# Operands of TensorE moved to multiples of 128 bytes, a few products left out, and a square root by ScalarE, in a one-core decoder layer

## The chip, the core and the metric

The kernel runs on one core of a Trainium2 chip. Its engines work side by side, each on its own list of instructions, and wait for one another by semaphores: TensorE (PE in the profile) multiplies matrices, with PEld for its weight loads; VectorE (DVE) and ScalarE (ACT) do elementwise work; GpSimd (POOL) does very little here; SyncE (SP) issues nearly all DMAs. Operands of TensorE lie in SBUF, a memory of 128 partitions, and its results go to PSUM. The metric is the time of one execution in microseconds (us) on the device.

## What is computed

One layer of a hybrid decoder, for one sequence of 2,048 tokens of width 1,024 in float32. The core of the reference:

```python
u = rmsnorm(h, norm_mix_w)
proj = u @ w_in                                  # hq, hf, hi, hg, attention's q, k, v
f = lb + (1 - lb) * sigmoid(hf);  k = 1 - f      # 4 heads, 128 x 128 state
# S_t = diag(f_t) S_{t-1} + k_t v_t^T,  o_t = S_t^T q_t, the state starts as zeros
o_hg = rmsnorm(o_hg, hg_norm_w) * silu(hg)
o_att = sliding_window_attention_with_sinks(...) # 8 query heads, 2 key heads, window 128
h = h + concat(o_hg, o_att) @ w_out
v = rmsnorm(h, norm_ffn_w)
gate = causal_depthwise_conv(v @ w_gate) ;  h = h + (silu(gate) * (v @ w_up)) @ w_down
return rmsnorm(h, final_norm_w)
```

## The kernel before

**Stages.** The sequence is worked in two halves of 1,024 tokens (`hf` 0 and 1). Each half passes through four stages: mix (projections, recurrent heads, attention), the output projection, gate and up, and down. In time, by the profile: mix of half 0 to about 339 us, the output projection to 452, gate and up to 877, down to 1,086; in half 1 the output projection begins at 1,421, gate and up run from 1,534 to 1,959, down to 2,137, and the row blocks of the end to 2,172.

**Large products.** Every large product is made of three products of the type float32r: both factors are split into a high part (a rounded copy by ScalarE) and a low part (what is left, by VectorE), and hi·hi, hi·lo and lo·hi are added up in PSUM. Nearly all have 128 x 128 weights (the stationary operand, loaded by an LDWEIGHTS of its own for each matmul) and a moving operand of 128 x 512. `unit` (line 202) makes the projections, 48 matmuls in each of 52 units. `project_v` (lines 601 to 603) uses x as weights and moves 256 columns. Gate and up go two tiles at a time through `pair_unit` (lines 734 to 736), where seven products of quarters stand for eight (Strassen's scheme; 84 matmuls, 44 times); down does the same over 2,816 channels (lines 921 to 923), piece by piece (`prep_piece`).

**Small products.** The recurrent heads (`hgrn`) cut a half into eight chunks of 128 tokens. For each head they transpose K (`pkn`, line 541), make each chunk's update of the state from it (`pu`, line 548), run the state through the chunks on VectorE (`SS`, line 552; `state` holds what the half before left, line 587), and add for each chunk the product of ST with v (line 563) to that of Q with the state before the chunk (line 564). Attention makes its scores (`psc`, line 387, float32r, 256 columns) from query parts `qh`, `ql` and the keys `KS`. The other small products are plain float32; the trace shows each of those as two matmul records, and transposes as one.

**The end.** In half 1 the last product of down is made with rows of tokens as its output, so that the last RMSNorm can be done row block by row block (`last_rows`, four blocks `tb` of 128 tokens). Per block: ScalarE squares and sums (line 1034), VectorE forms the mean (`msr`), takes 1/sqrt from an integer first guess (lines 1038, 1039) and three Newton steps of two instructions (lines 1042, 1043), and scales the rows (line 1046), which a DMA writes out. For the last block ScalarE also scales `y1` (line 1050) by the same factor.

**Memory plan.** Pools are laid one behind another in SBUF, and each tile is rounded up to 32 bytes per partition. The constants begin at byte 2,176 with `nmw` (32 bytes), `ones` (512), `warm` (4, rounded to 32), `ident` (512), `state` (2,048), and end at 11,840; then come the pools x, w and h with tiles of 4,096 bytes, a pool of small tiles, and the pool of the stage. What follows from that, modulo 128 bytes:

| tiles | offset modulo 128 |
|---|---|
| XH, XL, xhd, xld, whi, wlo, hid, lod, the tiles of h; K, Q, ST, Kn, G, KS, V; nearly all of gate, up and down | 64 |
| `ga`: two slots of 2 + 1,024 float32 (4,104 bytes, rounded to 4,128) | 64 and 96 |
| `dd` of each half's first pair, behind the two slots of `ga` | 0 |
| v, SS, sc, qh, ql, po, pp: behind `F64`, a tile of 32 bytes | 32 |
| ones | 32 |

The tag `ga` holds the gate tiles, and it is borrowed twice: by the first pair of each half for Sh and Sl (their low part in the second slot), and by down for the weights of every third piece, `k % 3 == 1` (hi in the first slot, lo in the second; the profile calls them gad). In the same way `dd` holds the first pair's factor S4. Slices that a matmul takes from a tile start at multiples of 512 bytes, except in the levels of `hgrn`.

**Order.** Within each engine instructions run in the order in which they were issued. `ORDER` interleaves the steps of heads and attention by hand, `tc.issue_after` delays two places, and a planner (a scheduler that works with estimated costs) decides in the end which engine's instruction of which strand comes when.

Of the kernel before, what the change touches and what calls it, by code (L numbers as in the profile page):

```python
# [8 lines left out]
F32 = mybir.dt.float32  # L9
F32R = mybir.dt.float32r  # L10
U32 = mybir.dt.uint32
I32 = mybir.dt.int32
AF = mybir.ActivationFunctionType
ALU = mybir.AluOpType
# [3 lines left out]
P = 128  # L18
D = 1024
KT = D // P  # L20
S = 2048
HALF = 1024
NH = S // HALF
TT = HALF // P
# [6 lines left out]
EPS = 1e-6  # L31
PIECES = [2, 2, 2, 2, 2, 1]
OPS = ["B11", "T1", "B21", "T2", "T3", "B22", "T4"]
QUADS = ["A11", "A12", "A21", "A22"]
PRODUCTS = [("P1", "A11", "B11"), ("P5", "S1", "T1"), ("P6", "S2", "T2"), ("P3", "S4", "B22"),
            ("P7", "S3", "T3"), ("P2", "A12", "B21"), ("P4", "A22", "T4")]
AFTER = {2: 'po'}
ORDER = ("f0 q0 l0 qa0 v0 s0 sc0 w0 pv0 p0 f1 q1 l1 g0 pw0 w1 qa1 g1 sc1 f2 s1 q2 p1 qa2 m0 pv1 pw1 l2 v1 "
         "s2 sc2 f3 m5 q3 g2 p2 pv2 pw2 qa3 m6 m1 sc3 l3 m4 m2 s3 g3 pv3 p3 pw3").split()
UP_AFTER = 'T2'  # L40
LEVELS = [1, 2, 4, 8, 16, 32, 64]
# [7 lines left out]
def hymba_layer(ctx: ExitStack, tc: tile.TileContext, a: dict, out: bass.AP, rows_out: bass.AP):  # L49
    nc = tc.nc  # L50
# [6 lines left out]
    cp = pool("const")  # L57
# [18 lines left out]

    nmw = cp.tile([P, KT], F32, name="nmw")
    nc.scalar.dma_start(nmw, a["norm_mix_w"])
    ones = cp.tile([P, P], F32, name="ones")
    nc.vector.memset(ones, 1.0)  # L80
    warm = cp.tile([P, 1], F32, name="warm")
    nc.scalar.activation(warm, ones[:, 0:1], AF.Sigmoid)
# [4 lines left out]
    state = cp.tile([P, HG, P], F32, name="state")  # L87
    nc.vector.memset(state, 0.0)
    halo = cp.tile([P, FT, 2], F32, name="halo")
# [7 lines left out]
    marks = {}  # L97
# [350 lines left out]
    def hgrn(hf, h, X, invb, vs, WG, gates, mix, p, fu=None):  # L448

        fu = fu or unit(a["w_f"][h], X, "f")  # L450
        f = p.tile([P, HALF], F32, tag="f", name="f", bufs=2)
# [12 lines left out]
        Q = p.tile([P, HALF], F32, tag="Q", name="Q", bufs=2)  # L464
# [3 lines left out]
        ST = p.tile([P, TT, P], F32, tag="t4", name="ST", bufs=2)  # L468
# [23 lines left out]
        F = f  # L492
        for m in LEVELS:
# [26 lines left out]
            Fv = F.rearrange("p (b w) -> p b w", w=2)  # L520
            Fn = p.tile([P, nb], F32, tag=f"F{m}", name=f"F{m}", bufs=1)
            nc.vector.tensor_tensor(Fn, Fv[:, :, 0], Fv[:, :, 1], op=ALU.mult)
# [11 lines left out]
        v = vs[h]  # L534

        Kn = p.tile([P, TT, P], F32, tag="t4", name="Kn", bufs=2)
        for b in range(NB):
            pk = ps("hg", "pkn")
            for i in range(4):
                c = slice((b * 4 + i) * P, (b * 4 + i + 1) * P)  # L540
                nc.tensor.transpose(pk[:, i * P:(i + 1) * P], K[:, c], ident)
            nc.scalar.copy(Kn[:, 4 * b:4 * b + 4].rearrange("p a b -> p (a b)"), pk)
        SS = p.tile([P, TT, P], F32, tag="SS", name="SS", bufs=1)
        for b in range(NB):
            pu = ps("hg", "pu")
            for i in range(4):
                c = 4 * b + i
                marks["pu"] = nc.tensor.matmul(pu[:, i * P:(i + 1) * P], Kn[:, c], v[:, c], start=True, stop=True)
            for i in range(4):
                c = 4 * b + i  # L550
                prev = state[:, h] if c == 0 else SS[:, c - 1]
                nc.vector.scalar_tensor_tensor(SS[:, c], prev, F[:, c:c + 1], pu[:, i * P:(i + 1) * P],
                                               op0=ALU.mult, op1=ALU.add)
# [5 lines left out]
        for c in range(TT):  # L559
            cs = slice(c * P, (c + 1) * P)  # L560
            prev = state[:, h] if c == 0 else SS[:, c - 1]
            o = po[c // 4][:, c % 4 * P:(c % 4 + 1) * P]
            nc.tensor.matmul(o, ST[:, c], v[:, c], start=True, stop=False)
            marks["po"] = nc.tensor.matmul(o, Q[:, cs], prev, start=False, stop=True)
            nc.scalar.activation(on[:, c], o, AF.Square, accum_out=ss[:, c:c + 1])
# [8 lines left out]
        for b, bs in halves():  # L574
# [8 lines left out]
            if h == HG - 1:  # L583
                hi, lo = mix[h]
                nc.scalar.copy(hi[:, bs], g[:, bs])
                nc.vector.tensor_tensor(lo[:, bs], g[:, bs], hi[:, bs].bitcast(F32), op=ALU.subtract)
        nc.vector.tensor_copy(state[:, h], SS[:, TT - 1])
        yield
# [176 lines left out]
    def gate_up(hf, ops, hs, nxt, p):  # L765
# [5 lines left out]
        for pr in range(FT // 2):  # L771
            f0 = 2 * pr
            W, nxt = nxt, None
            ga = [p.tile([P, 2 + HALF], F32, tag="ga", name="ga", bufs=2) for _ in range(2)]

# [218 lines left out]
    def last_rows(hf, hh, st, fw, ready, pieces, p, then):  # L994
# [6 lines left out]
        def small(name):  # L1001
            return sp.tile([P, 1], F32, tag=name, name=name)

        for tb in range(4):
            ts = slice(tb * P, (tb + 1) * P)
# [30 lines left out]
            nc.vector.tensor_scalar(ms, ss, 1.0 / D, base[:, tb:tb + 1], op0=ALU.mult, op1=ALU.add)  # L1036
            yi = y.bitcast(I32)
            nc.vector.tensor_scalar(yi, ms.bitcast(I32), 1, None, op0=ALU.logical_shift_right)
            nc.vector.tensor_scalar(yi, yi, -1.0, float(0x5F3759DF), op0=ALU.mult, op1=ALU.add)
            nc.vector.tensor_scalar(mh, ss, -0.5 / D, half[:, tb:tb + 1], op0=ALU.mult, op1=ALU.add)  # L1040
            for _ in range(3):
                nc.vector.tensor_scalar(t, y, y, mh, op0=ALU.mult, op1=ALU.mult)
                nc.vector.tensor_scalar(y, t, 1.5, y, op0=ALU.add, op1=ALU.mult)
# [131 lines left out]
```

## Time and profile before

| | us |
|---|---|
| time, median of 3 runs (2181.68 to 2183.84) | 2183.36 |
| the profiled execution | 2181.92 |
| its span, first to last instruction | 2179.9 |
| mean granted TensorE clock in it | 0.999 |

The page gives, for each engine, the busy time, its share of the span and the number of instructions; then the chain of work that ended last; then groups of instructions with their count, total and mean duration. Matmuls overlap each other: the duration of one (0.39 us for 512 columns) is longer than the distance from its start to the start of the next. How fast TensorE works is therefore read in the timeline, from start to start. For VectorE and ScalarE a duration is what an instruction costs, nearly.

### The profile page before, as it was taken

The page shows a single profiled execution, that of the slowest core. Times are in us where ns is not written, and L with a number is a line of the kernel's source. Part 1 is how long each engine was busy: PE and PEld are TensorE (multiplying, and loading weights), DVE is VectorE, ACT ScalarE, POOL GpSimd, SP SyncE. Part 2 cuts the span into 40 slices and gives each one's busy share as a digit, 9 for nine tenths or more (in the row PEclk, how much of TensorE's full clock was granted, in tenths as well). Part 3 has the DMA queues.
Part 4 walks back from the last instruction along what each step waited for, and adds up shares of the span by engine and source line. Part 5 has one row for each costly group of instructions (what it writes and reads, how often), then busy time and mean ns, then how long its engine had stood idle before and what let it go on. Part 6 is the DMA issues. An engine that isn't in the chain of part 4 may idle for free.

```text
span 2179.9 us, 29020 instructions
## 1 busy us (share of the span) xinstructions
PE 2162.5 (99%) x11211; PEld 1813.3 (83%) x11211; DVE 1630.9 (75%) x2458; ACT 1049.7 (48%) x1825; POOL 15.8 (1%) x37
## 2 busy tenths in 40 slices
PE   8999999999999999999999999999999999999998
PEld 7988988888888888888889889888888888888887
DVE  6566668689787878785865666677888888787865
ACT  6445456554444445335635365445644444443452
POOL 2000000000000000000000000000000000000000
PEclk9999999999999999999999999999999999999999
DMA  4111112413232334964641010114232323259743
GB/s 156 40 30 39 30 39 69 135 59 126 92 115 93 99 118 152 384 227 152 205 135 30 30 49 22 50 61 143 70 116 87 129 84 124 86 190 393 232 145 131
DMA packets 91146, 254.41 MB, mean 117 GB/s; under 512 B 11136, under 2 KB 13952, under 8 KB 91008
## 3 DMA queue, kind: packets, MB, share of 16 engines
q1 hardware_dynamic: 90576, 252.29, 34.6%
q8 instruction: 88, 1.44, 0.3%
q14 instruction: 50, 0.41, 0.1%
q10 hardware_dynamic: 432, 0.27, 0.0%
HBM read 195.37 MB, written 57.15 MB: 116 GB/s over the span
## 4 chain that ended last, share of the span: by engine, by line
PE 97%; DVE 1%; ACT 1%; DMA 1%; issue 0%; SPq 0%; DVEq 0%
PE pop L202 8%; PE X L734 7%; PE X L735 7%; PE X L736 7%; PE q L202 4%; PE g L202 4%; PE f L202 4%; PE hq L202 4%; PE Y L735 4%; PE Y L734 4%; PE Y L736 4%; PE pdx L922 3%; PE pdx L921 3%; PE pdx L923 3%; PE pdy L922 3%; PE pdy L921 3%
## 5 line engine op out<-in xcount | busy, mean ns | idle before, releaser
L609 ACT CAST whi<-raw 128x1024 fp32r<-128x1024 f32 x88 | 92.6, 1053 | 103.1 <-PE X L735 68.5
L805 DVE SCALAR_TENSOR_TENSOR y<-ga,cw,y 128x1024 f32<-128x1024 f32 x88 | 112.6, 1282 | 37.7 <-ACT y L803 37.7
L736 PE MATMUL X<-T,wlo 128*128 128x512 f32 x352 | 137.0, 389 | 0.0
L735 PE MATMUL X<-T,whi 128*128 128x512 f32 x352 | 136.9, 389 | 0.0
L734 PE MATMUL X<-T,whi 128*128 128x512 f32 x352 | 136.9, 389 | 0.0
L610 DVE TENSOR_TENSOR wlo<-raw,whi 128x1024 fp32r<-128x1024 f32 x88 | 107.5, 1221 | 5.7 <-ACT whi L609 5.7
L183 ACT CAST whi<-raw 128x1024 fp32r<-128x1024 f32 x58 | 60.6, 1050 | 102.6 <-PE g L202 22.4
L740 ACT COPY u<-X 128x512 f32<-128x512 f32 x88 | 51.8, 588 | 97.8 <-PE X L736 97.7
L610 DVE TENSOR_TENSOR xld<-raw,xhd 128x1024 fp32r<-128x1024 f32 x72 | 81.1, 1133 | 8.1 <-ACT xhd L609 7.9
L609 ACT CAST xhd<-raw 128x1024 fp32r<-128x1024 f32 x72 | 69.5, 979 | 32.5 <-DMA raw<-act1B 9.6
L202 PE MATMUL pop<-XH,wlo 128*128 128x512 f32 x256 | 83.7, 392 | 0.8 <-DVE wlo L184 0.8
L202 PE MATMUL pop<-XL,whi 128*128 128x512 f32 x256 | 83.8, 391 | 0.0
L202 PE MATMUL pop<-XH,whi 128*128 128x512 f32 x256 | 83.4, 396 | 0.2
L184 DVE TENSOR_TENSOR wlo<-raw,whi 128x1024 fp32r<-128x1024 f32 x58 | 70.4, 1218 | 12.3 <-ACT whi L183 12.3
L734 PEld LDWEIGHTS X<-T,whi 128*128 128x128 f32 x352 | 66.1, 188 | 13.8
L735 PEld LDWEIGHTS X<-T,whi 128*128 128x128 f32 x352 | 66.1, 188 | 13.7
L736 PEld LDWEIGHTS X<-T,wlo 128*128 128x128 f32 x352 | 66.1, 188 | 13.7
L740 ACT COPY s<-X 128x512 f32<-128x512 f32 x44 | 25.9, 590 | 106.3 <-PE X L736 106.3
L602 PE MATMUL pvv<-whi,XL 128*128 128x256 f32 x256 | 73.5, 289 | 0.0
L601 PE MATMUL pvv<-whi,XH 128*128 128x256 f32 x256 | 73.1, 287 | 0.0
L603 PE MATMUL pvv<-wlo,XH 128*128 128x256 f32 x256 | 72.1, 284 | 0.0
L734 PE MATMUL X<-T,Sh 128*128 128x512 f32 x176 | 68.7, 390 | 0.0
(389 smaller groups left out, 6555.6 us busy)
## 6 DMA issues: line engine op xcount, KB each, us to landing
wr<-in_w_down SPq DMA_DIRECT2D x90, 512.0 KB, 5.3
raw<-in_w_gate SPq DMA_DIRECT2D x44, 512.0 KB, 3.6
raw<-in_w_up SPq DMA_DIRECT2D x44, 512.0 KB, 3.6
raw<-act0T SPq DMA_DIRECT2D x20, 512.0 KB, 5.7
raw<-act1T SPq DMA_DIRECT2D x20, 512.0 KB, 5.0
act0B<-y SPq DMA_DIRECT2D x33, 256.0 KB, 2.3
act1B<-y SPq DMA_DIRECT2D x33, 256.0 KB, 2.2
raw<-in_w_out SPq DMA_DIRECT2D x16, 512.0 KB, 3.6
```

The lines of the kernel that those rows point to most:

```text
L202: nc.tensor.matmul(o[b], w, x[:, bs], start=f, stop=l)
L601: nc.tensor.matmul(o[:, 0:256], xh[:, t], hi[:, c], start=kt == 0, stop=False)
L602: nc.tensor.matmul(o[:, 0:256], xl[:, t], hi[:, c], start=False, stop=False)
L609: nc.scalar.copy(h, src)
L610: return (eng or nc.vector).tensor_tensor(l, src, h.bitcast(F32), op=ALU.subtract)
L734: nc.tensor.matmul(o, wh[:, ws], xh, start=i == 0 and not more, stop=False, skip_group_check=more)
L735: nc.tensor.matmul(o, wh[:, ws], xl, start=False, stop=False, skip_group_check=more)
L736: nc.tensor.matmul(o, wl[:, ws], xh, start=False, stop=i == 3, skip_group_check=more)
L740: nc.scalar.copy(t, o)
L805: nc.vector.scalar_tensor_tensor(y, g[:, w:w + HALF], C.cw[:, ft, w:w + 1], y, op0=ALU.mult, op1=ALU.add)
L921: nc.tensor.matmul(o, wh[:, i, c], ah[:, i, cols], start=f, stop=False, skip_group_check=more)
L922: nc.tensor.matmul(o, wh[:, i, c], al[:, i, cols], start=False, stop=False, skip_group_check=more)
```

## The change

The four edits, in the order of the diff. (1) `nmw` and `warm` become larger, so that the constants grow by 192 bytes and every pool behind them moves to 0 modulo 128; `F64` becomes 64 bytes instead of 32, and the tiles behind it move to 0 as well; the gate tiles become 1,056 float32 (4,224 bytes, 33 times 128), so that the second slot of `ga`, and `dd` behind it, lie at 0 modulo 128 too. `ones` moves to 64. (2) In half 0 the first chunk has an empty state: its product with the state, the memset of the state and the multiplication of the empty state are left out. (3) In half 1 nothing follows the last chunk: its transpose, its update and the copy to `state` are left out. (4) In `last_rows` the first guess comes from a square root by ScalarE and a reciprocal by VectorE, with one Newton step behind it instead of three; a square root of a constant ahead of the blocks brings ScalarE's table for it. `UP_AFTER` only moves within the file.

```diff
+GA = 1056
...
-    nmw = cp.tile([P, KT], F32, name="nmw")
+    nmw = cp.tile([P, 16], F32, name="nmw")[:, 0:KT]
...
-    warm = cp.tile([P, 1], F32, name="warm")
+    warm = cp.tile([P, 48], F32, name="warm")[:, 0:1]
...
-    nc.vector.memset(state, 0.0)
...
-            Fn = p.tile([P, nb], F32, tag=f"F{m}", name=f"F{m}", bufs=1)
+            Fn = p.tile([P, max(nb, 16)], F32, tag=f"F{m}", name=f"F{m}", bufs=1)[:, 0:nb]
...
+        kept = TT if hf + 1 < NH else TT - 1
...
-            for i in range(4):
+            n = min(4, kept - 4 * b)
+            for i in range(n):
                 c = slice((b * 4 + i) * P, (b * 4 + i + 1) * P)
                 nc.tensor.transpose(pk[:, i * P:(i + 1) * P], K[:, c], ident)
-            nc.scalar.copy(Kn[:, 4 * b:4 * b + 4].rearrange("p a b -> p (a b)"), pk)
+            nc.scalar.copy(Kn[:, 4 * b:4 * b + n].rearrange("p a b -> p (a b)"), pk[:, 0:n * P])
...
-            for i in range(4):
-                c = 4 * b + i
+            for c in range(4 * b, min(4 * b + 4, kept)):
+                i = c % 4
                 marks["pu"] = nc.tensor.matmul(pu[:, i * P:(i + 1) * P], Kn[:, c], v[:, c], start=True, stop=True)
-            for i in range(4):
-                c = 4 * b + i
+            for c in range(4 * b, min(4 * b + 4, kept)):
+                i = c % 4
+                if hf == 0 and c == 0:
+                    nc.vector.tensor_copy(SS[:, 0], pu[:, 0:P])
+                    continue
...
-            nc.tensor.matmul(o, ST[:, c], v[:, c], start=True, stop=False)
-            marks["po"] = nc.tensor.matmul(o, Q[:, cs], prev, start=False, stop=True)
+            empty = hf == 0 and c == 0
+            marks["po"] = nc.tensor.matmul(o, ST[:, c], v[:, c], start=True, stop=empty)
+            if not empty:
+                marks["po"] = nc.tensor.matmul(o, Q[:, cs], prev, start=False, stop=True)
...
-        nc.vector.tensor_copy(state[:, h], SS[:, TT - 1])
+        if hf + 1 < NH:
+            nc.vector.tensor_copy(state[:, h], SS[:, TT - 1])
...
-            ga = [p.tile([P, 2 + HALF], F32, tag="ga", name="ga", bufs=2) for _ in range(2)]
+            ga = [p.tile([P, GA], F32, tag="ga", name="ga", bufs=2)[:, 0:2 + HALF] for _ in range(2)]
...
+        nc.scalar.activation(warm, ones[:, 0:1], AF.Sqrt)
         for tb in range(4):
...
-            yi = y.bitcast(I32)
-            nc.vector.tensor_scalar(yi, ms.bitcast(I32), 1, None, op0=ALU.logical_shift_right)
-            nc.vector.tensor_scalar(yi, yi, -1.0, float(0x5F3759DF), op0=ALU.mult, op1=ALU.add)
+            nc.scalar.activation(t, ms, AF.Sqrt)
+            nc.vector.reciprocal(y, t)
...
-            for _ in range(3):
+            for _ in range(1):
```

More of the change, by code (lines that the diff above doesn't have):

```diff
@@ L37 @@
 AFTER = {2: 'po'}
+UP_AFTER = 'T2'
 ORDER = ("f0 q0 l0 qa0 v0 s0 sc0 w0 pv0 p0 f1 q1 l1 g0 pw0 w1 qa1 g1 sc1 f2 s1 q2 p1 qa2 m0 pv1 pw1 l2 v1 "
          "s2 sc2 f3 m5 q3 g2 p2 pv2 pw2 qa3 m6 m1 sc3 l3 m4 m2 s3 g3 pv3 p3 pw3").split()
-UP_AFTER = 'T2'
 LEVELS = [1, 2, 4, 8, 16, 32, 64]
```

## The prediction

> **What bounds the kernel now.** I read the page first: the shares by engine and the chain that ended last.
>
> ```profile
> span 2179.9 us, 29020 instructions
> ...
> PE 2162.5 (99%) x11211; PEld 1813.3 (83%) x11211; DVE 1630.9 (75%) x2458; ACT 1049.7 (48%) x1825; POOL 15.8 (1%) x37
> ...
> PE 97%; DVE 1%; ACT 1%; DMA 1%; issue 0%; SPq 0%; DVEq 0%
> ```
>
> TensorE (PE) is busy for 99% of the span and makes 97% of the chain; DVE, the next, has a quarter of the span free. The stages, in the view of busy time by window (columns: window, its length, then busy time and instructions of PE, PEld, DVE, ACT, POOL), say the same:
>
> ```profile
> 0.00:448.00 448.00, 440.62 (x2751) 376.99 (x2752) 304.60 (x560) 231.48 (x512) 15.82 (x37) 1.00 0.22 68
> ...
> 600.00:800.00 200.00, 200.00 (x884) 165.64 (x884) 166.72 (x213) 87.19 (x125) 0.00 (x0) 1.00 0.31 102
> ...
> 1086.00:1540.00 454.00, 451.31 (x2829) 387.07 (x2828) 309.35 (x577) 232.48 (x519) 0.00 (x0) 1.00 0.21 65
> ...
> 1950.00:2180.00 230.00, 222.53 (x995) 182.47 (x993) 163.75 (x239) 94.64 (x118) 0.00 (x0) 0.99 0.65 227
> ```
>
> In gate and up (600 to 800) no nanosecond of PE is idle. So only what PE executes, and its pace from one matmul to the next, can move the time; the exception is the last few microseconds. A busy PE says nothing of that pace, because the 389 ns that the page gives one matmul overlaps its neighbours. I therefore read start times, in the timeline of PE (start, duration, what). First the down projection, where hi/lo weights lie in the tiles "hid" and "lod":
>
> ```profile
> 919.91 0.39 PE L921 MATMUL pdy<-xhd,hid 128*128 128x512 f32 x1
> ...
> 922.63 0.39 PE L921 MATMUL pdy<-xhd,hid 128*128 128x512 f32 x1
> ```
>
> Twelve matmuls lie between these starts: 2.72 us, 226.7 ns each, or 0.68 us for a triple (hi·hi, lo·hi, hi·lo). Next the same code where the weights lie in the two slots of the tag "ga" (gad), and the count of gad's matmuls in the whole span (busy time by window, for this tile alone):
>
> ```profile
> 926.03 0.39 PE L921 MATMUL pdy<-xhd,gad 128*128 128x512 f32 x1
> ...
> 931.62 0.40 PE L921 MATMUL pdy<-xhd,hid 128*128 128x512 f32 x1
> ```
>
> ```profile
> 0.00:2180.00 2180.00, 149.79 (x624) 117.01 (x624) 31.79 (x26) 27.33 (x26) 1.00 0.35 117
> ```
>
> Twenty-four matmuls in 5.59 us: 233 ns each, 0.70 us for a triple. Engines, shapes and neighbours are the same; only the place of the weights differs. By the memory plan of the program (front part: moving operands and most weights at 64 modulo 128 bytes), the gad slots are at 64 (hi) and 96 (lo). Last, the first pair's "dd", whose weights alone lie at 0 modulo 128 while the moving operand stays at 64:
>
> ```profile
> 470.28 0.40 PE L734 MATMUL Y<-B,dd 128*128 128x512 f32 x1
> ...
> 473.08 0.39 PE L734 MATMUL X<-T,whi 128*128 128x512 f32 x1
> ```
>
> Twelve in 2.80 us: 233 ns again, although these are the weights that sit on a multiple of 128. What costs 6.7 ns here looks like weights that are *out of step with the moving operand*, not weights off a multiple of 128. Everything below hangs on that reading, and it isn't proved.
>
> **The change part by part.** All terms are on PE's path unless I say so, and the sum is taken from the profiled execution, 2181.92 us (span 2179.9; the median of the three timed runs, 2183.36, lies 1.4 above).
>
> *Padding: gad.* 624 matmuls are 208 triples; each gives back 0.70 − 0.68 = 0.02 us if both slots come into step: **−4.1 us**. Ends: 0 if the new distance of the slots (4,224 bytes, 128 more than a whole 4,096) is still out of step, and −4.1. Offsets of 32 and 64 are what the trace shows out of step, and 128 isn't shown; I take −4.1, since a period of 128 is the simplest that fits.
> The Trainium skill, page "TensorE: Matmul & The Clock Gate", section "Step-by-step: what each phase is for", says that loading the next weights takes no read bandwidth from the running matmul. By that rule the place of the weights could not matter and this term would be 0; the gad rows differ from it by 6 ns a matmul, so the trace doesn't bear it out.
>
> *Padding: the first pair's tiles.* S1 and S2 (8 triples a half, low part at 96) and dd (4 triples a half) make 24 triples at 0.02 us: **−0.5 us**.
>
> *Padding: everything that was already in step* (about 7,300 products at 512 columns, both operands at 64) moves by the same distance. I cost it at nothing; the ends are in the rivals.
>
> *Padding: attention's scores.* Here query tiles at 32 meet keys at 64; after it both are at 0. The price of in-step products at 256 columns is that of the v projection:
>
> ```profile
> 200.52 0.28 PE L387 MATMUL psc<-KS,qh 128*128 128x256 f32 x1
> ...
> 201.45 0.63 PE L202 MATMUL hq<-XH,wlo 128*128 128x512 f32 x2
> ```
>
> ```profile
> L387 PE MATMUL psc<-KS,qh 128*128 128x256 f32 x120 | 33.1, 300 | 0.0
> ...
> L387 PE MATMUL psc<-KS,ql 128*128 128x256 f32 x120 | 30.3, 282 | 0.0
> ```
>
> ```profile
> 69.87 0.28 PE L601 MATMUL pvv<-whi,XH 128*128 128x256 f32 x1
> ...
> 71.78 1.07 PE L502 MATMUL plev<-Q,G 128*128 128x128 f32 x8
> ```
>
> Eight scores take 0.93 us, 116 ns each; sixteen products of v take 1.91 us, 119 ns. 240 times 3 to 4 ns: **+0.9 us** (ends 0 and +1.0). The other tiles at 32 (v, SS, sc, po, pp) serve plain fp32 matmuls; pu (v at 32) and po from state (64) below run at the same pace, so they cost nothing either way.
>
> *Products that go.* Half 0 loses chunk 0's product with the state (4 heads, 2 passes each), half 1 loses the last chunk's transpose (4) and update (4 heads, 2 passes):
>
> ```profile
> L564 PE MATMUL po<-state,Q 128*128 128x128 f32 x16 | 3.1, 275 | 0.0
> ...
> L541 PE MATMUL pkn<-ident,K 128*128 128x128 f32 x64 | 8.9, 272 | 0.0
> ...
> L548 PE MATMUL pu<-v,Kn 128*128 128x128 f32 x128 | 16.9, 279 | 1.1 <-ACT Kn L542 1.1
> ```
>
> ```profile
> 376.47 0.39 PE L564 MATMUL po<-state,Q 128*128 128x128 f32 x2
> 376.69 0.39 PE L563 MATMUL po<-v,ST 128*128 128x128 f32 x2
> ```
>
> Two passes take 0.22 us from start to start. 8 + 4 + 8 = 20 passes at 0.11 us: **−2.2 us**. Their companions on DVE and ACT (four state copies, four updates turned into copies, shorter evictions of Kn) lie beside a PE that is never short there and count nothing. The memset of the state at the start was hidden too: DVE idles 2.46 us after the memsets, waiting for ACT.
>
> ```profile
> 1.12 0.48 DVE L88 MEMSET state<- 128x512 f32 x1
> ...
> 4.40 0.79 DVE L293 TENSOR_TENSOR wlo<-raw,whi 128x512 fp32r<-128x512 f32 x1 [2.46 <-ACT whi L292]
> ```
>
> *The root by ScalarE.* Only the fourth row block is on the path; the first three run beside matmuls. Its chain, in the timeline of DVE and ACT after the last matmul, and two rows for the new operations:
>
> ```profile
> 2173.00 0.19 ACT L1034 ACTIVATION_READ_ACCUMULATOR sqr<-rows 128x1 f32 x1
> ...
> 2173.36 0.21 DVE L1036 TENSOR_SCALAR msr<-ssr,base 128x1 f32<-128x1 f32 x1
> ...
> 2173.99 0.27 DVE L1042 TENSOR_SCALAR tr<-yr,mhr 128x1 f32<-128x1 f32 x1
> ...
> 2175.41 0.21 DVE L1043 TENSOR_SCALAR yr<-tr,yr 128x1 f32<-128x1 f32 x1
> ...
> 2175.66 0.91 ACT L1050 ACTIVATE y<-y,yr 128x256 f32<-128x256 f32 x2 [2.47 <-DVE yr L1043]
> ```
>
> ```profile
> L413 DVE RECIPROCAL den<-den 128x8 f32<-128x8 f32 x16 | 3.2, 202 | 0.4
> ...
> L82 ACT ACTIVATE warm<-ones 128x1 f32<-128x1 f32 x1 | 0.2, 203 | 0.0
> ...
> L807 ACT ACT_TABLE_LOAD x2 | 2.6, 1283 | 0.0
> ```
>
> From msr to the use of y it takes 2175.66 − 2173.36 = 2.30 us. New: msr 0.21, a hop to ACT, root 0.20, a hop back, reciprocal 0.20, and one step (2175.66 − 2175.10, 0.56). For a hop the trace has 0.04 (yr's end to ACT's start) and 0.17 (ACT's end at 2173.19 to msr); with both, 1.4 us: **−0.9 us** (ends −1.0 and −0.5). During the hop DVE has only mhr waiting, and that fits. The added wait on ACT holds up only y1's scaling, which needs the root anyway. The table load, 1.28 us, stands ahead of the row blocks, where ACT is busy 94.64 of 230 us; it costs nothing there. If Square or Identity needed another table than Sqrt, the last block would load one or two more, +1.3 to +2.6 us.
>
> *Order.* A planner puts the instructions of the heads in order, and with 20 passes gone it will interleave them somewhat differently. PE idles 448 − 440.62 = 7.4 us in the first mix stage (most of it before the first data) and 2.7 in the second, so I allow ±2.
>
> Sum: −4.1 − 0.5 + 0.9 − 2.2 − 0.9 = −6.8, so 2175.1 by the profiled execution; by the median of the timed runs 2176.6. I say **2176**.
>
> **The rivals.** *Not in step after all, or given back (chance 0.22).* The distance of 4,224 bytes doesn't cure gad, or the planner's new order eats about as much. Then −6.8 + 4.1 + 0.3 leaves −2.4, and with the order's ±2 **2180**. For it: no row has slots 128 bytes apart. Against it: 32 and 64 modulo 128 behave alike.
>
> *A multiple of 128 is worth more than being in step (0.14).* At 226.7 ns a matmul takes 13.3 ns more than these rows from the start, where the same product runs at a slower pace:
>
> ```profile
> 7.12 0.63 PE L202 MATMUL kv<-XL,whi 128*128 128x512 f32 x1
> ...
> 8.40 0.63 PE L202 MATMUL kv<-XH,wlo 128*128 128x512 f32 x1
> ```
>
> Three matmuls take 1.28 us, 427 ns each; at twice that pace it would be 213.3. The 13.3 ns left over are 32 of 512 columns, that is 128 bytes of the moving operand, and the v product's 119 to 120 ns leave the same over half of 213.3. A moving operand that starts in the middle of a 128-byte piece touches one piece more, 17 for 16; if that is the excess, all 512-column products (8,040 by the loops: 52 units of 48, 44 pairs of 84, 1,716 in down and 132 in the rows) drop 13.3 ns, −107 us, and 768 products of v some 8 ns, −6: **2065**. Against it: the scores start at 64 too and take 116 ns, less than the nine pieces at 13.3 ns that this account would need; and dd, with one operand on the multiple, is slower, not faster. In the Trainium skill, the same page, section "Wait — 56ns, not 53.3ns?", gives 215.7 ns from start to start for 512 columns at full clock; by that figure the estimate would be some 88 us less than before, and no run here shows it.
>
> *Slower (0.06).* dd's weights are the only ones on a multiple of 128, and its products take 233 ns. If that is due to the multiple itself and not to being out of step, all 8,040 products go from 226.7 to 233.3: +53, less the 3 us that the other parts give, **2232**. It decides as soon as whi and wlo move to 0 modulo 128 with the moving tiles, in every stage at once. Against it: gad's lo slot (96) loses just as much, and only one weight in three is there.
>
> **How the numbers follow.** Forecast 0.58, gad not cured or given back 0.22, aligned pieces 0.14, slower 0.06. The forecast's own range is 2172 to 2181 (root, order and hops); with the second case and 2 us of scatter between executions 2169 to 2186, which leaves out the last two, 0.2. About 0.2% (4.4 us) is what a measurement of this kernel can tell from no change; the forecast lies 7 below the median, so some four fifths of it counts as faster (0.47), all of the aligned pieces (0.14) and a fifth of the second case (0.04): faster 0.65. Same: 0.11 and 0.16, together 0.27. Slower 0.08.
>
> **What would show it.** In the changed kernel's profile: gad's triples at 0.68 us like hid's (step right) or 0.70 (wrong); dd the same; hid, whi and the rest still 226.7 ns from start to start, 884 matmuls in 200 us of gate and up. If this pace changes, my reading of the offsets is wrong, down to 213 for the pieces, up to 233 for the multiple, and the whole forecast with it. Twenty passes fewer (11,191 on PE); msr to y 1.4 us; one table load more. Scores at 119 to 120 ns.

## The result, and the profile after

| | before | after |
|---|---|---|
| time, median of 10 runs each (us) | 2182.27 (2181.68 to 2184.05) | 2177.11 (2175.95 to 2179.37) |
| the profiled execution | 2181.92 | 2175.99 |
| its span | 2179.9 | 2174.0 |

The ratio is 0.9974 (95%: 0.9966 to 0.9982), a gain of 5.2 us by the medians and 5.9 by the profiled executions. The forecast was 2176. Its total came out, but its terms did not: the largest, for gad, was 2.9 us too large, and that for the products left out 1.4 us too small. The page of the kernel after, the lines that answer to those of before:

```profile
span 2174.0 us, 28950 instructions
...
PE 2158.4 (99%) x11191; PEld 1812.3 (83%) x11191; DVE 1624.2 (75%) x2429; ACT 1044.9 (48%) x1828; POOL 13.8 (1%) x37
...
PE 99%; DVE 1%; DMA 0%; issue 0%; ACT 0%; SPq 0%; DVEq 0%; ACTq 0%
```

The bound is the same engine. TensorE has the 20 instructions fewer that were counted (11,211 to 11,191), and its busy time falls by 4.1 us while the span falls by 5.9. The other 1.8 us are idle time of TensorE: some 1.1 went behind the last matmul, which the prediction had priced as the root, another 1.1 went with a wait in half 1 (below), which it had not priced, and the start took 0.4 longer. Busy time by window, in gate and up:

```profile
600.00:800.00 200.00, 200.00 (x884) 165.60 (x883) 166.65 (x213) 86.82 (x125) 0.00 (x0) 1.00 0.31 102
```

It is again 884 matmuls in 200 us. Moving both operands of some 7,300 products together from 64 to 0 modulo 128 changed nothing. Now the rows on which the forecast hung: gad's first matmul and the first one behind its 24, in the timeline of PE (start, duration, what), then gad alone over the whole span (window, its length, then busy time and instructions of PE, PEld, DVE, ACT):

```profile
925.69 0.39 PE L929 MATMUL pdy<-xhd,gad 128*128 128x512 f32 x1
925.91 0.40 PE L930 MATMUL pdy<-xld,gad 128*128 128x512 f32 x1
...
931.23 0.39 PE L929 MATMUL pdy<-xhd,hid 128*128 128x512 f32 x1
```

```profile
0.00:2175.00 2175.00, 148.87 (x624) 117.78 (x624) 31.71 (x26) 27.26 (x26) 1.00 0.35 117
```

Twenty-four matmuls in 5.54 us are 231 ns each, where 226.7 was forecast and 233 was the case before. The same for the first pair's dd:

```profile
470.20 0.39 PE L742 MATMUL Y<-B,dd 128*128 128x512 f32 x1
...
472.92 0.39 PE L742 MATMUL X<-T,whi 128*128 128x512 f32 x1
```

Twelve in 2.72 us, 226.7 ns each: dd is cured and gad is not. The chain of the last row block, in the timeline of all engines:

```profile
2168.71 0.21 DVE L1045 TENSOR_SCALAR msr<-ssr,base 128x1 f32<-128x1 f32 x1 [0.60 <-ACT sqr L1043]
2168.84 0.20 DVE L1048 TENSOR_SCALAR mhr<-ssr,half 128x1 f32<-128x1 f32 x1
2168.96 0.20 ACT L1046 ACTIVATE tr<-msr 128x1 f32<-128x1 f32 x1 [0.28 <-DVE msr L1045]
2169.20 0.16 DVE L1047 RECIPROCAL yr<-tr 128x1 f32<-128x1 f32 x1
2169.40 0.27 DVE L1050 TENSOR_SCALAR tr<-yr,mhr 128x1 f32<-128x1 f32 x1
2169.70 0.21 DVE L1051 TENSOR_SCALAR yr<-tr,yr 128x1 f32<-128x1 f32 x1
2169.95 0.91 ACT L1058 ACTIVATE y<-y,yr 128x256 f32<-128x256 f32 x2 [0.79 <-DVE yr L1051]
```

From msr to y it takes 1.24 us instead of 2.30. Last, the whole mix stage of half 1, busy time by window, first before, then after:

```profile
1086.70:1421.40 334.70, 333.64 (x2168) 289.77 (x2169) 216.46 (x415) 168.02 (x378) 0.00 (x0) 1.00 0.18 55
```

```profile
1085.50:1418.07 332.57, 332.57 (x2160) 288.89 (x2159) 214.52 (x409) 161.45 (x374) 0.00 (x0) 1.00 0.18 55
```

Before, PE was idle for 1.06 of these 334.70 us; after, for none. The idle time had one place, in the timeline of PE, and one cause, in that of ACT:

```profile
1284.59 1.60 PE L548 MATMUL pu<-v,Kn 128*128 128x128 f32 x12 [1.05 <-ACT Kn L542]
```

```profile
1282.14 1.28 ACT L454 ACT_TABLE_LOAD   x1
1283.43 0.63 ACT L454 ACTIVATE f<-f 128x512 f32<-128x512 f32 x1
1283.97 1.06 ACT L542 COPY Kn<-pkn 128x512 f32<-128x512 f32 x2
```

The updates of the state waited for Kn, and the copy of Kn stood on ScalarE behind a table load. That load was the last of four within 10 us (from 1,273.92, 1,275.43, 1,277.37 and 1,282.14 us on), where functions of the heads (f) and of attention's softmax (es, sc) took turns; the kernel after has one in this place, at 1,274.9 us. In the kernel after, the same updates begin without a wait, between attention's scores:

```profile
1278.47 0.38 PE L550 MATMUL pu<-v,Kn 128*128 128x128 f32 x2
1278.60 0.36 PE L387 MATMUL psc<-KS,qh 128*128 128x256 f32 x1
...
1279.16 0.38 PE L550 MATMUL pu<-v,Kn 128*128 128x128 f32 x2
```

Where the time went, by stage: lengths in us, from the start of a stage's first matmul to that of the next one's, in each trace. (The start varies between executions: `pst`, the first sums of squares, comes at 30.7 to 31.6 us. So the first mix stage is taken from pst on. Down begins some 12 us before the last products of gate and up, which so count to down.) The last three columns are experiments of the next section.

| stage | before | after | gate tiles 256 apart | step at 64 | products only |
|---|---|---|---|---|---|
| mix, half 0, from pst | 308.64 | 308.22 | | | 308.17 |
| output projection 0 | 112.65 | 112.59 | 112.59 | 112.63 | 112.55 |
| gate and up 0 | 413.69 | 413.60 | 413.53 | 413.53 | 413.69 |
| down 0 | 220.99 | 220.01 | 218.55 | 218.55 | 220.67 |
| mix, half 1 | 334.77 | 332.54 | 332.54 | 334.65 | 332.37 |
| output projection 1 | 112.69 | 112.14 | 112.18 | 112.69 | 112.08 |
| gate and up 1 | 413.67 | 413.58 | 413.51 | 413.51 | 413.67 |
| down 1 | 189.55 | 188.97 | 187.69 | 187.69 | 189.55 |
| row blocks | 34.88 | 34.74 | 34.74 | 34.88 | 34.88 |
| last matmul to the end | 7.63 | 6.54 | 6.54 | 7.64 | 7.62 |

Down 0 takes 220.67 in all four experiments that leave it as it was; the 0.32 us more in the trace of before belong to that one execution.

### The profile page after: what moved, and what is told of

It is laid out like the page before. It is cut to its first block, busy times and chain, and to the rows that moved or that the text cites. A ratio compares the mean times of both kernels' runs of the same rounds, so it can differ in the third digit from the quotient of the medians.

```text
span 2174.0 us, 28950 instructions
## 1 busy us (share of the span) xinstructions
PE 2158.4 (99%) x11191; PEld 1812.3 (83%) x11191; DVE 1624.2 (75%) x2429; ACT 1044.9 (48%) x1828; POOL 13.8 (1%) x37
## 4 chain that ended last, share of the span: by engine, by line
PE 99%; DVE 1%; DMA 0%; issue 0%; ACT 0%; SPq 0%; DVEq 0%; ACTq 0%
PE pop L202 8%; PE X L742 7%; PE X L744 7%; PE X L743 7%; PE q L202 4%; PE hq L202 4%; PE g L202 4%; PE f L202 4%; PE Y L743 4%; PE Y L742 4%; PE Y L744 4%; PE pdx L931 3%; PE pdx L930 3%; PE pdx L929 3%; PE pdy L930 3%; PE pdy L931 3%
```

## The experiments

The question was why gad had kept most of its loss while dd had lost all of it, and which part gave the rest. My theory after the result: weights and moving operand have to be a multiple of 256 bytes apart, not of 128; the new slots are 4,224 bytes apart, 128 more than a multiple of 256. The rivals: gad is slow for another reason than its place; an operand on a multiple of 128 is worth something by itself; the gain comes from the products or from the root alone. Each kernel was timed together with the kernel before on the same chip; the medians of that one were 2181.95 to 2182.22.

**Gate tiles a multiple of 256 apart.** The kernel after, with one number changed (4,352 bytes, 17 times 256):

```diff
-GA = 1056
+GA = 1088
```

> The changed kernel with gate tiles of 1,088 instead of 1,056 float32, so that the second slot of ga lies 4,352 bytes behind the first, a multiple of 256, and not 4,224. Theory (weights out of step with the moving operand modulo 256 bytes cost time): gad's triples go from 0.693 to 0.680 us, 208 times 0.0133 = 2.8 us in the two down stages, and the first pair's Sl gives 0.2 more; some 2174.1 where the changed kernel has 2177.1. Rival (multiples of 128 are all that counts, and what is left of gad's cost comes from something else about these tiles): gad stays at 0.693, 2177.1.

Measured: 2174.77 us (2172.99 to 2175.2), ratio 0.9963 (0.9951 to 0.9976). The timeline of PE at gad, and gad alone over the whole span:

```profile
925.16 0.39 PE L929 MATMUL pdy<-xhd,gad 128*128 128x512 f32 x1
...
930.60 0.39 PE L929 MATMUL pdy<-xhd,hid 128*128 128x512 f32 x1
```

```profile
0.00:2172.00 2172.00, 146.14 (x624) 117.10 (x624) 31.78 (x26) 27.27 (x26) 1.00 0.35 117
```

Twenty-four matmuls in 5.44 us, 226.7 ns each: the loss is gone. By busy time gad goes from 149.79 us before to 148.87 after to 146.14 here, so by this measure the change had reached a quarter of what there was (0.92 of 3.65); by the lengths of the two down stages it is 1.2 of 4.0. By its span, 2171.1 us, this version is 2.9 below the kernel after and 8.8 below the kernel before; by the medians, taken in different sets of runs, 2.3 below the kernel after.

**The step alone, with everything left at 64 modulo 128.** The kernel before, with one line changed:

```diff
-            ga = [p.tile([P, 2 + HALF], F32, tag="ga", name="ga", bufs=2) for _ in range(2)]
+            ga = [p.tile([P, 1088], F32, tag="ga", name="ga", bufs=2)[:, 0:2 + HALF] for _ in range(2)]
```

> The kernel before with only the gate tiles changed, to 1,088 float32: every operand stays at 64 modulo 128, none moves to a multiple of 128, but the two slots of ga, and dd behind them, are now in step with the moving operands modulo 256. Theory (being in step is what counts): gad's triples 0.680 us as hid's, dd 226.7 ns a matmul, 4.1 + 0.5 us less than the kernel before, about 2177.7. Rival (a multiple of 128 is what counts): gad stays at 0.70, dd slow or unchanged, 2182.3.

Measured: 2178.01 us (2177.52 to 2179.83), ratio 0.9981 (0.9972 to 0.9990). The timeline of PE at gad and at dd:

```profile
926.00 0.39 PE L921 MATMUL pdy<-xhd,gad 128*128 128x512 f32 x1
...
931.44 0.39 PE L921 MATMUL pdy<-xhd,hid 128*128 128x512 f32 x1
```

```profile
470.83 0.39 PE L734 MATMUL Y<-B,dd 128*128 128x512 f32 x1
...
473.55 0.39 PE L734 MATMUL X<-T,whi 128*128 128x512 f32 x1
```

5.44 and 2.72 us: 226.7 ns each in both, with no operand of these products on a multiple of 128. Against the usual 220.67 and 189.55, the two down stages lose 2.1 and 1.9 us, 4.0 together. That is the −4.1 of the prediction, which the padding of the change had not bought. One line without a moved pool gives 4.2 us by the medians.

**The padding alone.** All the padding of the change (`nmw`, `warm`, `F64`) in the kernel before, with the gate tiles at 1,088; it differs from the kernel of the step alone only in where everything lies.

```diff
-    nmw = cp.tile([P, KT], F32, name="nmw")
+    nmw = cp.tile([P, 16], F32, name="nmw")[:, 0:KT]
...
-    warm = cp.tile([P, 1], F32, name="warm")
+    warm = cp.tile([P, 48], F32, name="warm")[:, 0:1]
...
-            Fn = p.tile([P, nb], F32, tag=f"F{m}", name=f"F{m}", bufs=1)
+            Fn = p.tile([P, max(nb, 16)], F32, tag=f"F{m}", name=f"F{m}", bufs=1)[:, 0:nb]
```

> The kernel before with only the padding of the change, and gate tiles of 1,088 float32: every pool at 0 modulo 256 and the slots in step. Theory (being in step counts, the multiple itself adds nothing; only the scores, now in step, change a little): the same as the run with gate tiles alone, about 2178.0, within 0.5. Rival (the multiple of 128 adds something of its own over all large products): clearly below 2178, by 1 us or more, and a pace below 226.7 ns in gate and up.

Measured: 2178.04 us (2177.02 to 2180.73), ratio 0.9982 (0.9973 to 0.9991), the same as the step alone. The multiple of 128 adds nothing that these runs can tell.

**The scores left out of step.** The first of these kernels (1,088) without the padding of `F64`, so that the query tiles lie 32 bytes off again:

```diff
-            Fn = p.tile([P, max(nb, 16)], F32, tag=f"F{m}", name=f"F{m}", bufs=1)[:, 0:nb]
+            Fn = p.tile([P, nb], F32, tag=f"F{m}", name=f"F{m}", bufs=1)
```

> The changed kernel with gate tiles of 1,088 float32 and without the padding of F64, so that qh, ql, v, SS and sc stay 32 bytes out of step with the keys and with K and Q. Theory (scores at 256 columns are the one place where out of step was cheaper, 117 against 119 ns, 240 matmuls; the large products next to them are dearer): within 0.5 us of the run with both paddings, 2174.8. Rival (the tiles at 32 cost the plain products something): 1 us or more above it.

Measured: 2174.26 us (2172.98 to 2174.67) beside the 2174.77 above; the ranges cover each other. What the scores cost is below what a time can tell here. Their own rows in the traces do tell it: from the start of each score to the start of what follows it, the scores take 0.14 us less in half 0 and 0.15 less in half 1 than with both paddings, some 0.3 together.

**Places, one against another.** A program of its own: 37 blocks of 48 float32r matmuls each, in which only the start of the moving operand (m) and of the weights (w) is shifted by so many bytes.

```
w0 = ws[i % len(ws)] // 4 + 128 * (i % 8)
m0 = m // 4 + 512 * (i % 2)
nc.tensor.matmul(o[:, 0:n], W[:, w0:w0 + P], M[:, m0:m0 + n], start=i == 0, stop=i == N - 1)
```

> Leaves the layer out: 48 float32r matmuls in a row on two loaded tiles for each of 37 placements; the moving operand and the weights are shifted by given bytes from a multiple of 512, weights change at each matmul as in the kernel. Theory (only the difference of the two addresses modulo 256 counts): 226.7 ns from start to start at differences of 0, 256 and 384-128 only if both move; 233 at 32 and 64; slower than 226.7 at 128; both shifted by the same 4 to 256 bytes: 226.7; the same whether weights or moving operand is the one shifted. Rival (a moving operand off a multiple of 128 touches one piece more): 213 to 216 wherever the moving operand is at 0, 128 or 256, 227 at 32 and 64, whatever the weights do. At 256 columns: 120 in step by the theory, 107 to 112 by the rival; 116 to 117 with weights 32 bytes off.

Measured in one execution (407.97 us). The timeline of PE joins a block into one row: its start, the time to the end of its last matmul, and in the name the shifts (m, w) and the columns (n); three numbers behind w are weights that take turns.

```profile
66.69 11.36 PE L43 MATMUL m0w64n512x<-M,W 128*128 128x512 f32 x48
...
89.13 11.32 PE L43 MATMUL m0w128n512x<-M,W 128*128 128x512 f32 x48
...
133.68 11.05 PE L43 MATMUL m0w256n512x<-M,W 128*128 128x512 f32 x48
...
189.39 11.15 PE L43 MATMUL m64w0n512x<-M,W 128*128 128x512 f32 x48
...
222.47 11.38 PE L43 MATMUL m4w4n512x<-M,W 128*128 128x512 f32 x48
...
255.80 11.07 PE L43 MATMUL m64w64n512x<-M,W 128*128 128x512 f32 x48
266.70 11.09 PE L43 MATMUL m128w128n512x<-M,W 128*128 128x512 f32 x48
...
288.51 11.35 PE L43 MATMUL m0w0w0w32n512x<-M,W 128*128 128x512 f32 x48
...
310.81 11.27 PE L43 MATMUL m0w0w0w128n512x<-M,W 128*128 128x512 f32 x48
...
333.01 11.04 PE L43 MATMUL m0w0w0w256n512x<-M,W 128*128 128x512 f32 x48
343.89 5.91 PE L43 MATMUL m0w0n256x<-M,W 128*128 128x256 f32 x48
349.64 5.84 PE L43 MATMUL m0w32n256x<-M,W 128*128 128x256 f32 x48
```

A row less the 0.39 us of its last matmul, divided by 47, is the distance from start to start: 11.05 gives 227 ns, 11.36 gives 233. Between the starts of 30 matmuls in the middle of each block, free of the borders:

| shift of moving operand, of weights (bytes), 512 columns | ns from start to start |
|---|---|
| 0, 0; 0, 256; 256, 0; 32, 32; 64, 64; 128, 128; 256, 256 | 226.7 |
| 0, 32; 0, 64; 0, 96; 0, 128; 0, 160; 0, 192; 0, 224; 0, 384 | 233.3; 233.3; 234.3; 232.3; 233.3; 228.9; 233.3; 232.7 |
| 4, 0; 16, 0; 32, 0; 64, 0; 128, 0 | 236.7; 231.5; 233.3; 228.9; 232.3 |
| 4, 4; 16, 16 | 233.3; 233.3 |
| 0 with 0, 0 and 32 in turn; with 64; with 128; with 192; with 256 | 233.3; 231.0; 231.2; 230.6; 226.7 |

Two things decide, as far as places were tried: weights and moving operand must differ by a multiple of 256, and both must lie on multiples of 32 (shifted together by 4 or 16 they are slow, by 32 and more they are not). Where they lie otherwise made no difference in any place tried. Two parts of the theory missed: shifting both by the same 4 or 16 bytes did not give 226.7, and it does matter which operand is shifted, as the difference has a sign (the moving operand shifted by 64 gives 228.9, like weights shifted by 192; weights shifted by 64 give 233.3). Why the step is 256 no run shows. The rows "in turn" are gad's own case, two weights in step and one out of it: 32 bytes off as before gives 233.3 (the kernel: 233), 128 off as after 231.2 (231), 256 off 226.7 (226.7).

The loss isn't spread evenly over the three. With 32 off, the distances from start to start of one triple are 232, 240 and 228 ns, in the scan and in the kernel before alike. In the kernel the out-of-step weights are those of line 923; their load, then the matmul before theirs and their own, in the timeline of before:

```profile
927.66 0.19 PEld L923 LDWEIGHTS pdy<-xhd,gad 128*128 128x128 f32 x1
```

```profile
927.65 0.40 PE L922 MATMUL pdy<-xld,gad 128*128 128x512 f32 x1
927.89 0.39 PE L923 MATMUL pdy<-xhd,gad 128*128 128x512 f32 x1
```

The load of the out-of-step weights begins with the matmul before theirs, and that matmul has the 240 ns: 13 of the 20 ns that a triple loses. Five fall on the first matmul of the triple, and why they do isn't shown.

**Products alone.** The kernel before with edits 2 and 3 (the empty state, the last chunk) and none of the others; its core:

```diff
+        kept = TT if hf + 1 < NH else TT - 1
...
+            empty = hf == 0 and c == 0
```

> The kernel before with only the left-out products (parts 2 and 3 of the change), no padding, no root by ScalarE. Theory (PE is the bound in both mix stages, 20 passes at 0.11 us go): 2.2 us less, 0.9 of it in half 0 and 1.3 in half 1; about 2180.1. Rival (in half 0 something else takes the place of the 8 passes, as the changed kernel's first mix stage is as long as before; in half 1 the whole gain): nothing in half 0, 1.3 to 2.8 in half 1, 2179.5 to 2181.

Measured: 2178.24 us (2177.95 to 2179.71), ratio 0.9981 (0.9972 to 0.9990). By the table of stages it takes 0.47 and 0.10 us off mix and output projection of half 0, and 2.40 and 0.61 off those of half 1: 3.6, more than the theory and the rival allowed. To tell the halves apart, each was then done by itself.

**Only the empty state of half 0.**

```diff
+        kept = TT
...
+            empty = hf == 0 and c == 0
```

> The kernel before with only the products with the empty state left out (half 0, 8 passes of PE; the memset of the state goes with them). Theory (each pass that goes is 0.11 us on PE's path): 0.9 us less from the first row sums to the output projection in half 0 (308.6 before), nothing in half 1. Rival (as the run with both parts shows 0.5 there): the new order of the heads gives half of it back, 0.4 to 0.6. In half 1 PE's wait of 1.05 us for the transposed keys at about 1,284 us stays, by both.

Measured: 2180.88 us (2180.66 to 2182.47), ratio 0.9992 (0.9983 to 1.0001). That interval still holds no change. Half 0 loses 0.47 and 0.09 us in the trace: from start to start the products po take 0.84 us less, close to the forecast, and the new order gives 0.28 back, 0.23 of it in the rows of other products and 0.05 in waits. That nothing changes in half 1 can't be read here: its mix is 336.19 us long, 1.4 more than before, since for 3.4 us from 1,099.3 us on the trace shows a granted clock of 0.50, and matmuls of 512 columns 427 ns apart. The wait of half 1 is still there, in the timeline of PE:

```profile
1285.48 2.05 PE L550 MATMUL pu<-v,Kn 128*128 128x128 f32 x16 [1.03 <-ACT Kn L544]
```

**Only the last chunk of half 1.**

```diff
+        kept = TT if hf + 1 < NH else TT - 1
...
+            empty = False
```

> The kernel before with only the last chunk's transpose, update and state copy left out in half 1 (12 passes of PE). Theory: 12 times 0.11 is 1.3 us, and with it goes PE's one long wait of that stage, 1.05 us for the transposed keys (Kn) behind a table load on ScalarE, because the planner puts the instructions in another order; together 2.3 to 2.9 us less in half 1's mix stage and output projection, nothing in half 0. Rival (the wait is unrelated to this part): 1.3 us less, and the wait stays.

Measured: 2178.92 us (2178.31 to 2181.15), ratio 0.9984 (0.9976 to 0.9993). Mix of half 1 takes 332.37 us and its output projection 112.11, 3.0 less than before together; nothing changes in half 0. The updates start without a wait, between the scores, as in the kernel after:

```profile
1279.38 0.38 PE L551 MATMUL pu<-v,Kn 128*128 128x128 f32 x2
1279.52 0.36 PE L388 MATMUL psc<-KS,qh 128*128 128x256 f32 x1
```

So the wait goes with the last chunk's products and not with the state's: with fewer instructions in the strand the planner comes to another order, and ScalarE has 24 table loads in the whole kernel instead of 28. It is a by-product: the waiting pu is the first of its head, and only the last chunk's was removed.

**The root alone.** The kernel before with edit 4:

```diff
+        nc.scalar.activation(warm, ones[:, 0:1], AF.Sqrt)
...
+            nc.scalar.activation(t, ms, AF.Sqrt)
+            nc.vector.reciprocal(y, t)
...
-            for _ in range(3):
+            for _ in range(1):
```

> The kernel before with only the square root by ScalarE in the last rows. Theory (the chain of the last block is the only place where it counts): 1.1 us less behind the last matmul, from 2.30 to 1.24 us between the mean and the use of the root, nothing elsewhere; about 2181.2. Rival (the table load or the added wait costs on the way): less than 0.5 us or nothing gained, an idle stretch of PE in the row blocks.

Measured: 2180.69 us (2179.92 to 2183.58), ratio 0.9994 (0.9985 to 1.0002), an interval that still holds no change. The trace shows the gain where the times can't: the timeline of the last block has

```profile
2173.65 0.21 DVE L1037 TENSOR_SCALAR msr<-ssr,base 128x1 f32<-128x1 f32 x1 [0.60 <-ACT sqr L1035]
...
2174.88 0.91 ACT L1050 ACTIVATE y<-y,yr 128x256 f32<-128x256 f32 x2 [0.79 <-DVE yr L1043]
```

1.23 us, the same as in the kernel after, and 6.68 us from the last matmul to the end instead of 7.63.

## Why the prediction was right, and where not

| term (us) | forecast | measured | from |
|---|---|---|---|
| gad | −4.1 | −1.2 | down 0 from the usual 220.67 to 220.01, down 1 from 189.55 to 188.97 |
| first pair's tiles | −0.5 | −0.2 | gate and up, 0.09 in each half |
| products in step already | 0 | 0 | 884 matmuls in 200 us |
| scores | +0.9 | +0.3 | mix and output projection of after less those of products only: 0.09 in half 0, 0.23 in half 1 |
| products that go | −2.2 | −3.6 | products only, four stages |
| root | −0.9 | −1.2 | after: last matmul to the end 1.09, row blocks 0.14 (root alone: 0.95 and 0.14) |
| sum | −6.8 | −5.9 | the profiled execution: −5.9 |

(Without the 0.3 us that only the trace of before had in down 0, the profiled executions are 5.6 apart; the very start took 0.4 us longer in that of after.)

**Gad: the failed step** is "a period of 128 is the simplest that fits". The reading in front of it, that weights out of step with the moving operand cost the 6.7 ns, was right: with the slots 256 apart in step, the kernel with everything at 64 gave 4.0 us. But the period is 256. With 32 and 64 as the only offsets in the trace of before, 128, 256 and more fitted equally well, and I took the smallest as certain enough to forecast by. The bound was there (0), and it stood among the rivals at 0.22; the measured term lies between the two cases, since 128 bytes cost 4.5 ns a matmul where 32 cost 6.7.

**First pair.** The right mechanism, and a size that was off by the same period: dd was cured, but S1 and S2 keep their low part in gad's second slot. In step throughout, gate and up lose 0.16 us in each half, 0.3 together, where 0.5 was forecast. The rest is S2: its four triples of a half alternate with products of another kind (ones, invb), and take 2.98 us before and 2.99 in step.

**In step already** was right: no pace changed. With that both rivals that made the multiple of 128 itself the cause fall, and the scan shows why: 64, 64 and 128, 128 both run at 226.7 ns. The time of the first (2065) and of the second (2232) would have needed 213 or 233. Here the Trainium skill, page "TensorE: Matmul & The Clock Gate", section "Wait — 56ns, not 53.3ns?", with its 215.7 ns for 512 columns, isn't what float32r with a weight load for each matmul shows in any place tried: the lowest was 226.7. And by the rule that the prediction weighed against gad, from the same page's section "Step-by-step: what each phase is for", by which the next weights' load takes nothing from the running matmul, all blocks of the scan would have run alike; they lie between 226.7 and 236.7 ns.

**Scores.** The sign was right, the size too large. The price in step, 119 ns, was right; the price before was read from eight scores, 116 ns, where the mean is 117.3 (from the second score of each uninterrupted run on, over the whole trace; after: 119.1). And the first score of a run does not get dearer, so that all scores together, from start to start, take 0.14 us more in half 0 and 0.15 in half 1 than in the trace of the products alone.

**Products that go.** The passes themselves were sized about right in sum: 3.6 less the wait of pu for Kn that left with them, 1.05, is 2.5 where 2.2 was forecast. By halves it was less good. Half 0 gave 0.6 of its 0.9: the passes went at 0.105 us each, 0.84, and the new order took 0.28 back, among it a wait of 0.10 us of PE for the levels of the heads (`plev`), which grew to 0.17. Half 1 gave, without the wait, 1.9 for its 1.3. The rows of the last chunk's run say where that comes from: pkn takes 0.43 us less for its 4 passes, pu 1.36 less for its 8, since the 56 that stay are 106 ns apart instead of 114 on average, and all other rows together 0.2 less. So the passes were priced about right, and the new order packs what stays closer; why pu gains by it isn't shown. What was missed is the wait. The page of before named it, in the row that the prediction quoted for pu: "1.1 <-ACT Kn L542". I read only its mean duration. It was covered by the ±2 allowed for the order, but as an uncertainty, not as a gain that a shorter strand could bring.

**Root.** Right to 0.2 us in the chain: msr to y is 1.24 instead of 1.4, since the hops took 0.04 each (2168.92 to 2168.96 and 2169.16 to 2169.20) where I had priced one at 0.17. The tables came out otherwise than said. "One table load more" was two fewer, 26 for 28: two came with the root (root alone: 30) and four went with the last chunk's products (24). The load meant to stand ahead of the row blocks was put by the planner at the very start, and Sqrt's table was loaded once more at its first use; the view of that line, then the timeline of ACT:

```profile
L1012 ACT ACT_TABLE_LOAD  x1: 1283/1283/1283, 2.8 to 2.8; - x1
```

```profile
2151.65 0.60 ACT L1043 ACTIVATE sqr<-rows 128x512 f32<-128x512 f32 x1 [3.74 <-PE rows L1041]
...
2152.36 1.28 ACT L1046 ACT_TABLE_LOAD   x1
2153.65 0.29 ACT L1046 ACTIVATE tr<-msr 128x1 f32<-128x1 f32 x2
```

So the preload did nothing. The real load fell beside the matmuls of the later row blocks, and it stayed for the rest: in the last block Square, Identity and Sqrt follow one another without another load, so the +1.3 to +2.6 that I had kept open did not come.

**The whole.** Two misses of opposite sign, +2.9 for gad and −1.4 for the products, leave a sum that is 0.9 off. That the time came out so close to the forecast is in good part luck, and shows little about the reasons; only the rows did.

## What to carry to other kernels

A matmul's pace is read from start to start, for each pair of operand tiles by itself; where the same shape runs at two paces, compare the places of weights and moving operand before anything else. For float32r with 512 columns they had to differ here by a multiple of 256 bytes, on multiples of 32, so pad the slots of a ring to a multiple of 256, and leave alone what is already in step. And where an engine is busy for 99%, the list of its few waits is worth a price each: an edit that only shortens a strand can move one away.

## What was not expected of the hardware

- One weight out of step slows its neighbours: with one in three 32 bytes off, the mean of all three is 233.3 ns, as high as with every one off. Most of it falls on the matmul before, beside which these weights are loaded (240 ns), little on their own (228).
- Operands shifted together by 4 or 16 bytes run at 233.3 ns, by 32 or more at 226.7: being in step does not help below 32.
- At 256 columns it is the other way round. In step takes 120.0 ns, out of step 116.5 to 118.7 (118.3 with the weights at 32). So scores are better left as they were, by an amount (some 0.3 us) that no time here could tell.
- The 13.3 ns over 213.3 (an estimate: half of the 427 ns that the start shows, and that the trace of half 0 alone shows again while the granted clock is 0.50) stay at every place tried where the operands are in step, and at 256 columns 13.3 over 106.7: a fixed amount for each matmul, not a matter of where its operands start. What they are isn't shown.
